# In-projection of a hybrid attention backbone: gates, keys and high parts on ScalarE instead of GpSimd

## Chip, core and metric

One core of one Trainium2 chip. The metric is the device time of one execution in microseconds (us), the median of several runs.

## What is computed

One layer of a diffusion backbone over 2048 latent tokens and 256 context tokens of width 1024, in float32. The part that matters here is the combined input projection and the gated scan (HGRN2) that reads four heads of it:

```python
p = modulate(x, norm1_g[l], sh1, sc1) @ w_in[l]
pc = modulate(ctx, norm1_g[l], csh1, csc1) @ w_in[l]

q = silu(p[..., O_HQ:O_HFF])
def gate(z, lb):
    f = lb + (1.0 - lb) * sigmoid(z)
    return 1.0 - f, log(f)
fwd = gate(p[..., O_HFF:O_HFB], lb_fb[0])
bwd = gate(p[..., O_HFB:O_HI], lb_fb[1])
```

f is the decay per token and channel, 1 - f is the key. There are two scans, one forwards and one backwards, each of four heads with 128 key channels and 64 value channels. Latent attention, a Fourier mixture, an output projection and a feed-forward network follow; they are not touched.

## The kernel before, in words

**Precision.** A float32 product is made from three TensorE products of a rounded format (mm3, lines 83 to 87): each operand is split into a high part, the rounded value, and a low part, what is left. Function hi (line 72) makes the high part, on the engine that it is given: a tensor_scalar with 1 and 0 on GpSimd (POOL), a copy on ScalarE (ACT), a copy on VectorE (DVE). Function lo (line 80) subtracts on DVE. So every weight (wraw, loaded by DMA) becomes wh and wl, and every modulated activation (xmt) becomes xh and xl.

**Stages.** The in-projection works in blocks: one of 256 context tokens (up to about 115 us in the profile), then four of 512 latent tokens (to about 898 us). For each block prep normalises the rows, transposes them on TensorE (ptx), lets ACT apply gain and shift (xmt, line 301) and splits the result, eight times for the eight slices of 128 features. The prep of the next block is emitted before the fourth head of the present one. Then come values and output gates (values_in, 512 columns), four heads (head_in, 384 columns each: query, forward gate, backward gate), the columns of attention (attention_in, 448) and of the Fourier mixture (fourier_in, 256). Weights come in pieces of at most 1536 columns of a tile (pieces, load_w): a latent block has ten pieces of 1536, two of 1344, three of 1024 and one of 896. There are two buffers of wh, two of wl and three of wraw; a new wh has to wait until TensorE has used the one before last.

**One head (hgrn).** ACT takes the sigmoids of the query and of the two gates out of PSUM. POOL then makes the gates, f = sigmoid x (1 - lb) + lb (line 369, one direction each), both keys at once, k = 1 - f (line 370, 1024 wide), and a second copy of f forwards (line 372). DVE makes q x f (line 377) and kd, the sum of the two keys (line 379). The scan over 128 tokens is then done by doubling, in seven levels m = 1, 2, 4, ... 64. In each of the first five ACT copies the keys of the level into ku (line 389), TensorE makes the level's scores psl from ku and q (line 394), and DVE puts them into pr and multiplies keys and queries by the decays of the level (lines 415 and 418), in place, for the next one. POOL multiplies the decays in pairs (tt, line 421), seven products, each half as wide as the one before. The last two levels use TensorE without a copy (pfin, lines 410 and 412). Then kt (transposed keys), pd (state increments), S (states) and po (output) follow. ACT also issues the DMAs that store dsb, q2 and ot.

**Order.** The tile framework plans the order of the instructions of each engine on its own, by the order of the program and by when it expects operands and buffers; nothing is written out by hand. Each engine works its queue in that order. In the trace the projection matmuls of the next head (accf) lie between the levels of the present one on TensorE.

**Who makes wh before.** For a latent block POOL, for the context block ACT (the argument eng of load_w). xh and the context's xch are made on POOL in both cases.

Of the kernel before, what the change touches and what calls it, by code (L numbers as in the profile page):

```python
# [13 lines left out]
AF = mybir.ActivationFunctionType  # L14
ALU = mybir.AluOpType
# [10 lines left out]
TB = 512  # L26
# [16 lines left out]
def tile_backbone(  # L43
# [6 lines left out]
    pe, act, dve, pool, sp = nc.tensor, nc.scalar, nc.vector, nc.gpsimd, nc.sync  # L50
# [21 lines left out]
    def hi(eng, dst, src):  # L72
        if eng is pool:
            pool.tensor_scalar(dst, src, 1.0, 0.0, ALU.mult, ALU.add)  # L74
        elif eng is act:
            act.copy(dst, src)  # L76
        else:
            dve.tensor_copy(dst, src)

    def lo(dst, src, h, eng=None):  # L80
        (eng or dve).tensor_tensor(dst, src, h, ALU.subtract)  # L81
# [32 lines left out]
    lbt = const.tile([P, 8], F32, name="lbt")  # L114
    omlb = const.tile([P, 8], F32, name="omlb")
# [6 lines left out]
    def rstd(rp, ssq, n, scale, name):  # L122

        m = rp.tile([P, 16], F32, tag="rs_m", name=name + "m")
        r = rp.tile([P, 16], F32, tag="rs_r", name=name + "r")
        pool.tensor_scalar(m[:, :n], ssq, scale, EPS, ALU.mult, ALU.add)
        pool.tensor_tensor(r[:, :n], m[:, :n], half[:, :n], ALU.pow)
        return r
# [94 lines left out]
    with p1 as ph:  # L223
# [17 lines left out]
        def load_raw(cols, n, k0, nk):  # L241
            raw = wp.tile([P, 1536], F32, tag="wraw", bufs=3, name="wraw")
            rv = raw[:, :nk * n].rearrange("p (k n) -> p k n", k=nk)
            o = 0
            for s, wd in cols:
                sp.dma_start(rv[:, :, o:o + wd],
                             w_in[0, k0 * P:(k0 + nk) * P, s:s + wd].rearrange("(k p) n -> p k n", p=P))
                o += wd
            return raw

        def pieces(n):
            step = min(4, 1536 // n)
            return [(k0, min(step, KT - k0)) for k0 in range(0, KT, step)]
# [7 lines left out]
            state[h] = b2.tile([P, 64], F32, tag=f"S{h}", bufs=6, name=f"S{h}_i")  # L261
            dve.memset(state[h], 0.0)

        def load_w(cols, n, k0, nk, eng):

            raw = early.pop((cols[0], k0), None)
            if raw is None:
                raw = load_raw(cols, n, k0, nk)
            wh = wp.tile([P, 1536], F32R, tag="wh", name="wh")
            wl = wp.tile([P, 1536], F32R, tag="wl", name="wl")  # L270
            hi(eng, wh[:, :nk * n], raw[:, :nk * n])
            lo(wl[:, :nk * n], raw[:, :nk * n], wh[:, :nk * n])
            return (wh[:, :nk * n].rearrange("p (k n) -> p k n", k=nk),
                    wl[:, :nk * n].rearrange("p (k n) -> p k n", k=nk))

        def prep(blk, xs):
            src, w, t0, T, bi = blk
            nt = T // P
            ssq = e2.tile([P, 4], F32, tag="ssq", name="ssq")
            for t in range(nt):  # L280
                junk = ea.tile([P, D], mybir.dt.bfloat16, tag="junk", name="junk")
                act.activation(junk, xs[t], AF.Square, accum_out=ssq[:, t:t + 1])
            r = rstd(e2, ssq[:, :nt], nt, 1.0 / D, "rx")
            for t in range(nt):
                dve.tensor_scalar(xs[t], xs[t], r[:, t:t + 1], None, ALU.mult)
            xh, xl = [], []
            per = TB // T
            bank = {}

            def step(k):  # L290
                if k % per == 0:
                    pp, tag = [(ps1, "tp"), (ps1, "ho"), (pss, "hs"), (pss, "hs")][0 if w == 0 else k // per]
                    if w == 0:
                        pp, tag = (pss, "hs") if k % 2 else (ps1, "tp")
                    bank[0] = pp.tile([P, TB], F32, tag=tag, name="ptx")
                pt = bank[0]
                po = k % per * T
                for t in range(nt):
                    pe.transpose(pt[:, po + t * P:po + (t + 1) * P], xs[t][:, k * P:(k + 1) * P], ident)
                xm = e2.tile([P, TB], F32, tag="xmt", name="xmt")  # L300
                act.activation(xm[:, :T], pt[:, po:po + T], AF.Identity, bias=modt[:, w, k:k + 1], scale=gain1[:, w, k:k + 1])
                if w == 0:
                    h = xmp.tile([P, TB], F32R, tag="xh", name="xh")
                    l = xmp.tile([P, TB], F32R, tag="xl", name="xl")
                else:
                    if k % 4 == 0:
                        bank[1] = e1.tile([P, 1024], F32R, tag=("zh", "zl")[k // 4], name="xch")
                    if k % 2 == 0 and k < 4:
                        bank[2] = e1.tile([P, 512], F32R, tag="uv", bufs=2, name="xcl")
                    if k == 4:  # L310
                        bank[2] = ea.tile([P, 1024], F32R, tag="pt", name="xcl2")
                    h = bank[1][:, k % 4 * CTX:(k % 4 + 1) * CTX]
                    l = bank[2][:, k % 2 * CTX:(k % 2 + 1) * CTX] if k < 4 else bank[2][:, (k - 4) * CTX:(k - 3) * CTX]
                hi(pool, h[:, :T], xm[:, :T])
                lo(l[:, :T], xm[:, :T], h[:, :T])
                xh.append(h)
                xl.append(l)
            return (xh, xl), [lambda k=k: step(k) for k in range(KT)]

        def token_major(xm, blk, cols):  # L320
            T = blk[3]
            n = sum(wd for _, wd in cols)
            acc = [psm.tile([P, 512], F32, tag="mm", name="acc") for _ in range(T // P)]
            for k0, nk in pieces(n):
                wh, wl = load_w(cols, n, k0, nk, pool if T == TB else act)
                for t in range(T // P):
                    for k in range(nk):
                        kk = k0 + k
                        ts = slice(t * P, (t + 1) * P)
                        mm3(acc[t][:, :n], xm[0][kk][:, ts], xm[1][kk][:, ts], wh[:, k, :], wl[:, k, :],  # L330
                            kk == 0, kk == KT - 1)
            return acc

        def feature_major(xm, blk, cols):
            T = blk[3]
            n = sum(wd for _, wd in cols)
            acc = [psm.tile([P, TB], F32, tag="mm", name="accf") for _ in range(n // P)]
            for k0, nk in pieces(n):
                wh, wl = load_w(cols, n, k0, nk, pool if T == TB else act)
                for f in range(n // P):  # L340
                    for k in range(nk):
                        kk = k0 + k
                        fs = slice(f * P, (f + 1) * P)
                        mm3(acc[f][:, :T], wh[:, k, fs], wl[:, k, fs], xm[0][kk][:, :T], xm[1][kk][:, :T],
                            kk == 0, kk == KT - 1)
            return acc

        def hgrn(blk, h, acc, vt):
            lat = blk[1] == 0
            T = blk[3]  # L350
# [8 lines left out]
            if lat:  # L359
                f3 = hp[h % 2].tile([P, 3, T], F32, tag="f3", name="f3")  # L360
                k2 = hp[h % 2].tile([P, 2, T], F32, tag="k2", name="k2")
            else:
                f3 = ea.tile([P, 2, T], F32, tag="rope", name="f3c")
                k2 = ea.tile([P, 2, T], F32, tag="junk", name="k2c")
            act.activation(f3[:, 0, :], pff[:, :T], AF.Sigmoid)
            act.activation(f3[:, 1, :], pfb[:, :T], AF.Sigmoid)
            for d in range(2):
                i = d * 4 + h
                pool.tensor_scalar(f3[:, d, :], f3[:, d, :], omlb[:, i:i + 1], lbt[:, i:i + 1], ALU.mult, ALU.add)
            pool.tensor_scalar(k2, f3[:, 0:2, :], -1.0, 1.0, ALU.mult, ALU.add)  # L370
            if lat:
                pool.tensor_scalar(f3[:, 2, :], f3[:, 0, :], 1.0, 0.0, ALU.mult, ALU.add)
                q = hp[h % 2].tile([P, T], F32, tag="q", name="q")
                act.activation(q, pq[:, :T], AF.Sigmoid)
                dve.tensor_tensor(q, pq[:, :T], q, ALU.mult)
                q2 = hp[h % 2].tile([P, 2, T], F32, tag="q2", name="q2")
                dve.tensor_tensor(q2, f3[:, 1:3, :], strided(q, 0, [[0, 2], [1, T]]), ALU.mult)
                kd = b1.tile([P, T], F32, tag="kd", name="kd")
                dve.tensor_tensor(kd, k2[:, 0, :], k2[:, 1, :], ALU.add)
                pr = b1.tile([P, TB], F32, tag="pr", name="pr")  # L380
# [196 lines left out]
        xm, steps = prep(blocks[1], x0)  # L577
# [28 lines left out]
        for n, blk in enumerate(blocks[1:]):  # L606
# [15 lines left out]
            if not end:  # L622
                xm = nxm
# [416 lines left out]
    with ExitStack() as ph:  # L1040
# [451 lines left out]
        for g, i in enumerate(begins):  # L1492
            n, ks = DORDER[g // len(DK)], DK[g % len(DK)]
# [77 lines left out]
```

## Time and profile before

| | |
|---|---|
| Median of 3 runs | 3284.93 us (3282.6 to 3285.95) |
| Profiled execution | 3281.53 us, span 3279.7 us |
| Granted TensorE clock, mean of the span | 0.982 |
| Busy: TensorE, VectorE, ScalarE, GpSimd | 95%, 65%, 37%, 24% |

In the views PE is TensorE (PEld its weight loads), DVE is VectorE, ACT is ScalarE, POOL is GpSimd. A busy time is the time in which an instruction of that engine was running. An idle time is shown in square brackets, with the instruction that ended it. "L394" is line 394 of the kernel. The granted clock is a share of 2.4 GHz; the other level is 1.2 GHz.

### The profile page before, as it was taken

Reading aid. Unit: us, or ns where it says so; the run is one execution under the profiler, and the core shown is the slowest. Engines: PE = TensorE matmul, PEld = TensorE weight load, DVE = VectorE, ACT = ScalarE, POOL = GpSimd, SP = SyncE. Lnnn points to the kernel's source line nnn. Section 1 sums busy time; section 2 is a strip of 40 time slices with the busy share of each in tenths; the row PEclk is TensorE's granted clock in tenths of the full one; section 3 lists DMA queues with packets and bytes.
Section 4 is the critical chain, followed back from the end, with each engine's and each line's share of the span. In section 5 each row is a group of like instructions: output and inputs, shape, how many; then the busy total and the mean of one; then the engine's idle time right before and its main releaser. Section 6 shows DMA issues by size and latency. Waiting matters only on the chain.

```text
span 3279.7 us, 45162 instructions
## 1 busy us (share of the span) xinstructions
PE 3101.9 (95%) x16770; PEld 2594.1 (79%) x16770; DVE 2135.6 (65%) x3354; ACT 1221.2 (37%) x2524; POOL 789.4 (24%) x784
## 2 busy tenths in 40 slices
PE   7998999999979999999999989999999999999987
PEld 5777777777758888888888877888878888888866
DVE  6675655656686767676656466766677666455765
ACT  3323122222225545555553334333343333343343
POOL 3433443424440111110101341111101111010534
PEclk9999999999989999999999989999999999999998
DMA  6523233133361212121105665533353333865562
GB/s 232 168 71 121 83 95 108 56 110 99 95 214 35 62 43 82 45 79 34 36 31 201 220 223 175 184 99 108 107 157 113 97 103 112 266 228 177 193 212 103
DMA packets 372609, 407.98 MB, mean 124 GB/s; under 512 B 50122, under 2 KB 240420, under 8 KB 371364
## 3 DMA queue, kind: packets, MB, share of 16 engines
q1 hardware_dynamic: 357748, 394.08, 37.9%
q10 hardware_dynamic: 13776, 8.92, 0.9%
q8 instruction: 132, 2.16, 0.3%
q0 software_dynamic: 864, 2.10, 0.2%
q14 instruction: 89, 0.73, 0.1%
HBM read 296.21 MB, written 108.79 MB: 123 GB/s over the span
## 4 chain that ended last, share of the span: by engine, by line
PE 53%; DMA 4%; DVE 3%; POOL 2%; ACT 1%; issue 1%; SPq 0%; POOLq 0%; DVEq 0%; ACTq 0%
PE sc L890 7%; PE dn L85 3%; PE dn L87 3%; PE dn L86 3%; PE y L87 3%; PE y L85 3%; PE y L86 3%; PE ptv L906 3%; PE z L85 2%; PE z L87 2%; PE z L86 2%; PE x L86 2%; PE x L87 2%; PE x L85 2%; PE po L87 1%; PE po L86 1%
## 5 line engine op out<-in xcount | busy, mean ns | idle before, releaser
L892 DVE TENSOR_REDUCE mx<-sc 128x1 f32<-128x512 f32 (+1 forms) x320 | 201.8, 631 | 123.0 <-PE sc L890 122.3
L1371 POOL TENSOR_TENSOR e<-e,e 128x512 f32<-128x512 f32 x44 | 91.3, 2076 | 751.1 <-ACT e L1370 689.6
L76 ACT CAST pth<-ptv 128x512 fp32r<-128x512 f32 x288 | 169.6, 593 | 234.9 <-PE ptv L906 228.2
L85 PE MATMUL dn<-wp,hdh 128*128 128x512 f32 x616 | 241.9, 393 | 6.4 <-ACT tmp L1472 5.2
L87 PE MATMUL dn<-wp,hdl 128*128 128x512 f32 x616 | 242.2, 393 | 5.0 <-DVE hdl L81 5.0
L86 PE MATMUL dn<-wp,hdh 128*128 128x512 f32 x616 | 241.4, 392 | 0.0
L81 DVE TENSOR_TENSOR ptl<-ptv,pth 128x512 fp32r<-128x512 f32 x288 | 196.2, 686 | 66.3 <-ACT pth L76 64.0
L898 ACT ACTIVATE p<-sc,mx 128x512 f32<-128x512 f32 (+1 forms) x320 | 201.9, 649 | 91.2 <-DVE mx L895 87.3
L85 PE MATMUL y<-xol,wp 128*128 128x512 f32 x528 | 207.7, 393 | 6.1 <-DVE xol L81 4.0
L86 PE MATMUL y<-xoh,wp 128*128 128x512 f32 x528 | 206.4, 391 | 0.0
L87 PE MATMUL y<-xoh,wp 128*128 128x512 f32 x528 | 205.7, 391 | 0.1
L81 DVE TENSOR_TENSOR wp<-wg,wp 128x512 fp32r<-128x512 f32 x176 | 127.3, 725 | 110.7 <-ACT wp L76 106.9
L81 DVE TENSOR_TENSOR wl<-wraw,wh 128x1536 fp32r<-128x1536 f32 (+3 forms) x78 | 118.6, 1521 | 118.5 <-POOL wh L74 117.3
L890 PE MATMUL sc<-kth,q 128*128 128x512 f32 (+1 forms) x640 | 194.6, 377 | 0.0
L87 PE MATMUL accf<-xh,wl 128*128 128x512 f32 x448 | 184.5, 412 | 10.3 <-DVE wl L81 10.3
L890 PE MATMUL sc<-kp,q 128*128 128x512 f32 (+1 forms) x640 | 190.4, 374 | 0.0
L85 PE MATMUL accf<-xl,wh 128*128 128x512 f32 x448 | 183.6, 410 | 0.0
L86 PE MATMUL accf<-xh,wh 128*128 128x512 f32 x448 | 182.9, 408 | 0.0
L906 PE MATMUL ptv<-ident,p 128*128 128x128 f32 x1152 | 178.7, 275 | 3.0 <-DVE ptl L81 1.5
L81 DVE TENSOR_TENSOR hdl<-hr,hdh 128x512 fp32r<-128x512 f32 x154 | 121.8, 803 | 84.9 <-ACT hdh L76 50.9
L85 PE MATMUL po<-ptl,ckh 128*128 128x256 f32 x576 | 169.1, 294 | 0.0
L76 ACT CAST hdh<-hr 128x512 fp32r<-128x512 f32 x154 | 94.4, 621 | 188.8 <-PE dn L86 145.0
(387 smaller groups left out, 8525.7 us busy)
## 6 DMA issues: line engine op xcount, KB each, us to landing
wg<-in_w_gate_up_dram SPq DMA_DIRECT2D x88, 512.0 KB, 4.8
hr<-hid SPq DMA_DIRECT2D x154, 256.0 KB, 3.9
wraw<-in_w_in_dram SPq DMA_DIRECT2D x112, 256.0 KB, 3.9
dw<-in_w_down_dram SPq DMA_DIRECT2D x97, 256.0 KB, 4.7
hid<-hs SPq DMA_DIRECT2D x66, 256.0 KB, 2.0
wm<-in_w_mod_dram SPq DMA_DIRECT2D x64, 256.0 KB, 2.7
hid<-e SPq DMA_DIRECT2D x44, 256.0 KB, 2.0
hid<-f SPq DMA_DIRECT2D x44, 256.0 KB, 3.3
```

Of the source, the lines that this page charges most:

```text
L76: act.copy(dst, src)
L81: (eng or dve).tensor_tensor(dst, src, h, ALU.subtract)
L85: pe.matmul(ps, ah, bl, start=first, stop=False, skip_group_check=more)
L86: pe.matmul(ps, ah, bh, start=False, stop=False, skip_group_check=more)
L87: pe.matmul(ps, al, bh, start=False, stop=last, skip_group_check=more)
L890: pe.matmul(s[:, :n], a[:, ts], bb[:, js], start=i == 0, stop=i == 4)
L892: dve.tensor_reduce(mx[:, j:j + 1], s[:, :n], AX.X, ALU.max)
L898: act.activation(u["p"][:, a:e], u["s"][i][:, :e - a], AF.Exp, bias=mx[:, 5:6], accum_out=mx[:, 6 + i:7 + i])
L906: pe.transpose(pt[:, i, u * P:(u + 1) * P], ps[u]["p"][:, (2 * g + i) * P:(2 * g + i + 1) * P], ident)
L1371: pool.tensor_tensor(e6, e6, e, ALU.add)
```

## The change

Every high part of the in-projection (wh, xh, xch), both gates, the keys and the copy of f are made by ACT, with the same values: the gates as an activation Identity with a scale and a bias per partition, the keys as Identity with scale -1 and bias 1. On POOL stay the products of the decays (tt) with their last copy, and the roots (rstd). Buffers, loads, matmuls and DVE's instructions are as before.

```diff
@@ -261,14 +261,14 @@
             state[h] = b2.tile([P, 64], F32, tag=f"S{h}", bufs=6, name=f"S{h}_i")
             dve.memset(state[h], 0.0)
 
-        def load_w(cols, n, k0, nk, eng):
+        def load_w(cols, n, k0, nk):
 
             raw = early.pop((cols[0], k0), None)
             if raw is None:
                 raw = load_raw(cols, n, k0, nk)
             wh = wp.tile([P, 1536], F32R, tag="wh", name="wh")
             wl = wp.tile([P, 1536], F32R, tag="wl", name="wl")
-            hi(eng, wh[:, :nk * n], raw[:, :nk * n])
+            hi(act, wh[:, :nk * n], raw[:, :nk * n])
             lo(wl[:, :nk * n], raw[:, :nk * n], wh[:, :nk * n])
             return (wh[:, :nk * n].rearrange("p (k n) -> p k n", k=nk),
                     wl[:, :nk * n].rearrange("p (k n) -> p k n", k=nk))
@@ -311,7 +311,7 @@
                         bank[2] = ea.tile([P, 1024], F32R, tag="pt", name="xcl2")
                     h = bank[1][:, k % 4 * CTX:(k % 4 + 1) * CTX]
                     l = bank[2][:, k % 2 * CTX:(k % 2 + 1) * CTX] if k < 4 else bank[2][:, (k - 4) * CTX:(k - 3) * CTX]
-                hi(pool, h[:, :T], xm[:, :T])
+                hi(act, h[:, :T], xm[:, :T])
                 lo(l[:, :T], xm[:, :T], h[:, :T])
                 xh.append(h)
                 xl.append(l)
@@ -322,7 +322,7 @@
             n = sum(wd for _, wd in cols)
             acc = [psm.tile([P, 512], F32, tag="mm", name="acc") for _ in range(T // P)]
             for k0, nk in pieces(n):
-                wh, wl = load_w(cols, n, k0, nk, pool if T == TB else act)
+                wh, wl = load_w(cols, n, k0, nk)
                 for t in range(T // P):
                     for k in range(nk):
                         kk = k0 + k
@@ -336,7 +336,7 @@
             n = sum(wd for _, wd in cols)
             acc = [psm.tile([P, TB], F32, tag="mm", name="accf") for _ in range(n // P)]
             for k0, nk in pieces(n):
-                wh, wl = load_w(cols, n, k0, nk, pool if T == TB else act)
+                wh, wl = load_w(cols, n, k0, nk)
                 for f in range(n // P):
                     for k in range(nk):
                         kk = k0 + k
@@ -366,10 +366,10 @@
             act.activation(f3[:, 1, :], pfb[:, :T], AF.Sigmoid)
             for d in range(2):
                 i = d * 4 + h
-                pool.tensor_scalar(f3[:, d, :], f3[:, d, :], omlb[:, i:i + 1], lbt[:, i:i + 1], ALU.mult, ALU.add)
-            pool.tensor_scalar(k2, f3[:, 0:2, :], -1.0, 1.0, ALU.mult, ALU.add)
+                act.activation(f3[:, d, :], f3[:, d, :], AF.Identity, bias=lbt[:, i:i + 1], scale=omlb[:, i:i + 1])
+            act.activation(k2, f3[:, 0:2, :], AF.Identity, bias=1.0, scale=-1.0)
             if lat:
-                pool.tensor_scalar(f3[:, 2, :], f3[:, 0, :], 1.0, 0.0, ALU.mult, ALU.add)
+                act.copy(f3[:, 2, :], f3[:, 0, :])
                 q = hp[h % 2].tile([P, T], F32, tag="q", name="q")
                 act.activation(q, pq[:, :T], AF.Sigmoid)
                 dve.tensor_tensor(q, pq[:, :T], q, ALU.mult)
```

## Rows read from the trace of the kernel before

**Rows 1.** The page, busy time of the engines (share of the span).

```profile
PE 3101.9 (95%) x16770; PEld 2594.1 (79%) x16770; DVE 2135.6 (65%) x3354; ACT 1221.2 (37%) x2524; POOL 789.4 (24%) x784
```

**Rows 2.** Stretches: busy us and count of each engine, granted clock, DMA share, GB/s.

```profile
100.00:900.00 800.00, 737.81 (x4591) 613.65 (x4589) 502.68 (x661) 193.02 (x396) 329.81 (x319) 0.98 0.34 99
...
280.00:290.00 10.00, 6.59 (x23) 4.91 (x21) 8.89 (x12) 2.61 (x4) 4.37 (x4) 0.66 0.55 176
...
350.00:360.00 10.00, 7.53 (x35) 6.10 (x35) 5.02 (x4) 1.45 (x2) 9.33 (x7) 1.00 0.40 110
...
550.00:560.00 10.00, 7.53 (x32) 6.17 (x30) 7.43 (x5) 2.39 (x4) 9.68 (x7) 0.83 0.28 79
```

**Rows 3.** TensorE's waits from 100 to 900 us: us in total, times, longest.

```profile
PE psl L394 <- ACT ku L389: 21.7, 13, 2.5
PE psl L394 <- DVE q L418: 15.6, 14, 1.8
PE accf L87 <- DVE wl L81: 10.3, 3, 3.5
PE pfin L410 <- DVE q L418: 4.0, 5, 0.9
```

**Rows 4.** All waits from 100 to 900 us, longest first.

```profile
POOL wh L74 <- PE acc L87: 148.6, 23, 24.2
...
POOL wh L74 <- PE accf L86: 92.7, 27, 6.5
...
ACT ku L389 <- POOL k L370: 60.9, 16, 5.2
```

**Rows 5.** POOL in order of time, one head: start us, us, engine, line, operation.

```profile
350.06 0.77 POOL L369 TENSOR_SCALAR f<-f,omlb,lbt 128x512 f32<-128x512 f32 x1 [4.83 <-ACT f L365]
...
351.90 1.49 POOL L74 TENSOR_SCALAR wh<-wraw 128x1536 fp32r<-128x1536 f32 x1 [0.37 <-PE accf L86]
353.37 2.34 POOL L369 TENSOR_SCALAR f<-f,omlb,lbt 128x512 f32<-128x512 f32 x1
355.80 2.08 POOL L370 TENSOR_SCALAR k<-f 128x1024 f32<-128x1024 f32 x1
357.85 1.46 POOL L421 TENSOR_TENSOR tt<-f 128x768 f32<-128x768 f32 x1
```

**Rows 6.** The same head on ACT, DVE and TensorE, in order of time.

```profile
352.07 0.60 ACT L366 ACTIVATE f<-accf 128x512 f32<-128x512 f32 x1 [2.12 <-PE accf L87]
...
353.42 1.82 DVE L81 TENSOR_TENSOR wl<-wraw,wh 128x1536 fp32r<-128x1536 f32 x1 [5.46 <-POOL wh L74]
...
355.75 1.22 DVE L377 TENSOR_TENSOR q<-f,q 128x1024 f32<-128x1024 f32 x1 [0.51 <-POOL f L369]
...
357.91 0.85 ACT L389 COPY ku<-k 128x512 f32<-128x512 f32 x1 [5.24 <-POOL k L370]
...
357.91 1.95 DVE L379 TENSOR_TENSOR kd<-k 128x512 f32<-128x512 f32 x1 [0.94 <-POOL k L370]
...
358.81 1.59 PE L394 MATMUL psl<-q,ku 128*128 128x128 f32 x8 [2.47 <-ACT ku L389]
...
364.83 0.68 DVE L418 TENSOR_TENSOR q<-q,tt 128x512 f32<-128x512 f32 x1
```

**Rows 7.** ACT's groups by shape, 0 to 960 us: busy us, mean ns, idle before.

```profile
L76 ACT CAST wh<-wraw 128x1024 fp32r<-128x1024 f32 x10 | 10.4, 1044 | 22.7 <-DMA wraw<-in_w_in_dram 17.4 <-PE accf L86 5.3
...
L76 ACT CAST wh<-wraw 128x768 fp32r<-128x768 f32 x4 | 3.3, 836 | 4.0 <-PE acc L87 2.4 <-PE accf L86 1.5
...
L301 ACT ACTIVATE xmt<-ptx,modt,gain 128x512 f32<-128x512 f32 x32 | 23.5, 776 | 35.8 <-DVE xl L81 32.7 <-PE ptx L299 2.6 <-DVE S L443 0.5
```

**Rows 8.** DVE and TensorE at the prep of the next block, in order of time.

```profile
280.53 1.55 DVE L491 TENSOR_SCALAR pt<-pt,rqr 128x256 f32<-128x256 f32 x1
...
282.26 0.34 DVE L491 TENSOR_SCALAR pt<-pt,rqr 128x256 f32<-128x256 f32 x1
...
284.38 0.80 PE L87 MATMUL accf<-xh,wl 128*128 128x512 f32 x1 [3.41 <-DVE wl L81]
```

## Prediction

> **What bounds the kernel now.** I read the page first: TensorE is busy for 95% of the span [rows 1], so time can only come back where TensorE stands still or runs slow. The change touches the in-projection alone, which lies between 100 and 900 us in the trace (its context block before that), so I went on to the table of stretches: over those 800 us TensorE is busy for 737.8, ScalarE (ACT) for 193, GpSimd (POOL) for 330 and VectorE (DVE) for 503 [rows 2]. No engine but TensorE is short of time. 62 us of TensorE are idle, and the granted clock is 0.98 in the mean, some 2% of 800 us, so 16 us more are lost to the lower of its two levels.
>
> Which waits make up the 62 us is in TensorE's own list of waits [rows 3]: the level products (psl) wait for the key copy ku on ACT, 21.7 us in 13 waits; psl and pfin wait for DVE's q products, 15.6 + 4.0 us; three times a projection waits for a low part of the weights (wl), 10.3 us. The list of all waits says what stands behind ku: ACT's 16 waits for POOL's k, 60.9 us [rows 4].
>
> One head shows the mechanism [rows 5, 6]. ACT's second sigmoid ends at 352.67. POOL has just begun a weight copy (wh, 351.90, 1.49 us), so the gate waits till 353.37. Then that gate takes 2.34 us, where the first one took 0.77 with the same shape: DVE's wl (two SBUF inputs) began at 353.42, and POOL finished only after it. The keys k take 2.08 us, half of that beside DVE's q product. At 357.88 the keys are there, ku follows, and psl starts at 358.81, after 2.47 us of idle TensorE. So the delay of the first level is POOL's queue and POOL's slow running beside DVE, and that is what the change takes out.
>
> **The change, part by part.** Durations are from the profiled execution of 3281.53 us (span 3279.7, so 1.8 us lie around it); the median of the runs is 3284.93, 3.4 above it. I work out a difference in the trace and take it off the median.
>
> *Gates and keys.* Per latent head ACT gets two gates (512 wide, scale and bias per partition, as xmt: 0.776 us [rows 7]), one key pass over 1024 (as wh 1024 wide: 1.044) and one copy of 512. The two rows of wh on ACT give 0.81 ns an element, so 512 cost 0.836 - 0.208 = 0.63 us. Behind the second sigmoid come one gate and the keys: 0.78 + 1.04 = 1.82 us, so the keys would be ready at 354.5, 3.4 us earlier; if ACT first has to do the wh copy (1536 wide: 1.044 + 512 x 0.81 ns = 1.46 us) they come at 356.0, still 1.9 earlier. psl of this level also needs DVE's q product, which stands behind wl: wl ends at 355.24, the product takes 1.22, so 356.5. psl can then start near 356.5 to 357.0 rather than 358.81: 1.8 to 2.3 us of a 2.47 gap, and all of the shorter ones. Of 21.7 us I take 19.
>
> *What is late next.* DVE. Its kd product starts at 357.91, right when the keys are there; now it could start at 356.46, when the q product ends: 1.45 us earlier. TensorE arrives up to 2.3 us earlier, so in the first head of each of the four blocks its next wait for q grows by 0.85: +3 us. In the others the two shifts are alike, or DVE gains more. Levels together: -16 us.
>
> *High parts of weights and activations.* By the code a latent block has 16 wh copies: ten of 1536, two of 1344, three of 1024, one of 896; with four blocks and 0.81 ns an element that is 85 us on ACT. 32 xh copies cost 32 x 0.63 = 20, the gates 32 x 0.78 = 25, the keys 17, the copies of f 10: 157 us on top of 193 in 800 us, 44%. The load itself is hidden by ACT's idle time; were that gone, each copy would stand in front of a ku. What the move gives is at the prep of the next block: up to 284.38 TensorE stands for 3.41 us for wl, which on DVE is queued behind the norms of queries and keys; one scaling there took 1.55 us, the next of its shape 0.34 [rows 8], and POOL was at a wh copy during the first. With POOL quiet 1.2 us go there, and some 0.7 in the products next to it (estimated from the same ratio): three such places, -6. The xl products of that stretch and the q products behind them run less slowly too: I take 1 us a block, -4.
>
> *Clock.* In 280 to 290, where the 3.41 us gap lies, the granted clock was 0.66, so much of it passed at the 1.2 GHz level; in 550 to 560 it was 0.83 with TensorE busy for 7.53 of 10 us; but 350 to 360 kept 1.00 with the same 7.53 [rows 2]. So a shorter gap may or may not give the clock back. Bounds: 0 and the whole 16 us. Since most dips lie behind gaps that go, but not all do, I take -8.
>
> *What it costs.* No DMA is moved, but ACT's queue also issues the stores of dsb, q2 and o, and these, sigmoids, ku and kt now stand behind wh copies that wait for TensorE to free a buffer. The trace has no such wait on ACT here. Below: 0, if the copy is always due when it comes up. Above: each of the 40 wide copies holds TensorE for its 1.46 us, 58 us. TensorE has projection matmuls of the next head between the levels, which cover about one copy, so I stay near the lower end: 4 copies, +6. In the context block eight copies of 256 (0.42 us each) now alternate with xmt on ACT, 3.4 us at most, part of it in ACT's waits for the transposes: +1. Fewer POOL instructions save nothing by themselves. Sum: -16 - 6 - 4 - 8 + 6 + 1 = -27, so 3258 us.
>
> **Rivals.** *The wait is handed on to DVE.* POOL keeps the decays' products (tt, 1.46 us and six smaller). In the trace DVE's kd, right beside the first of them, takes 1.95 us, a product of the same shape 0.68 when they are done [rows 5, 6]. They now start as soon as the gates are there, some 3 us earlier, onto wl and the q product; if these stretch by what kd does now (1.27), psl starts at 357.8, and with kd delayed alike the next wait eats what the first gives back. Then a head gains 1 us where the gap was 2.47 and hardly anything elsewhere, with no clock regained: 4 to 5 us in all, 3280. For it: DVE, not POOL, is behind 19.6 us of TensorE's waits [rows 3]. Against it: POOL's gates and keys are gone from the overlap. The Trainium skill ("GPSIMD Engine Reference", section Specifications) says that the two engines share their SBUF interfaces, with contention while a VectorE instruction has two SBUF inputs; by that rule this rival's overlap costs what the old one did, and the trace agrees for kd.
>
> *ACT's queue becomes the wait; slower.* POOL's wh stood 92.7 us in 27 waits for the projections of a head and 148.6 us in 23 for the other ones [rows 4]; there nothing was behind it that TensorE needed soon. On ACT a ku stands behind it. If a wh copy comes up before TensorE has freed its buffer, the ku behind it is late by the mean of those waits, 92.7 / 27 = 3.4 us, and TensorE with it. With one such hold in each of the 16 heads it is 55 us in place of my 6: -27 + 49 = +22, 3307. It decides from about ten holds, where the gain of 34 is used up. For it: one queue of ACT now carries both chains. Against it: a copy that is placed after the matmuls that free its buffer rarely waits long, and ACT is under half busy.
>
> *The change doesn't do what it says*: the order on the engines is planned anew, and the gaps come back elsewhere in equal size. Time as before, 3285.
>
> **How the numbers follow.** This kernel's measurement can tell about 0.2%, 6.6 us, from no change. Forecast: 0.66, from -50 (all 21.7, 10.3 and 16 us back) to -10. Handed on to DVE: 0.12, mostly within 0.2%, a little of it faster. ACT's queue: 0.17, slower. No effect: 0.05. Faster: 0.66 + 0.04 = 0.70; same 0.08 + 0.05 = 0.13; slower 0.17. The range goes from 3235 (-50) to 3290, which takes in the second and the fourth case and the mildest of the third, and leaves out some 0.15 above and a little below.
>
> **What would show it.** Right: ku waits for ACT's own keys for no time; TensorE's waits for ku fall from 21.7 us to under 5; idle TensorE in the in-projection falls from 62 to about 40 us, the granted clock rises; gates near 0.78 us, all alike; TensorE's waits for q near 20 us still; ACT near 350 us busy in the stage. Handed on: the waits for ku are gone and those for q have doubled. ACT's queue: TensorE waits for ku longer than before, and ku's releaser is no longer DVE's k but ACT itself, with wh waits for TensorE in front. The prediction is wrong if TensorE's idle time falls and the time does not, or if the time falls outside the in-projection.

## The result, and the profile after

The changed kernel takes 3235.96 us (median of 4 runs, 3230.5 to 3238.43) where the one before takes 3283.76 beside it (4 runs, 3280.25 to 3285.95): a ratio of 0.9843 [0.9824, 0.9862], 51.6 us of the 3284.93 that the prediction started from. The forecast was 3258, 27 us less, so the sign was right and the size was half of what came: 3233.4 by the ratio, just beyond the low end of the range, 3235. (The two medians by themselves lie 47.8 us apart, the two profiled executions 43.6.) The profiled execution of after took 3237.96 us, span 3236.2.

The page's line of busy times, against [rows 1]:

```profile
PE 3090.6 (96%) x16770; PEld 2592.0 (80%) x16770; DVE 2105.0 (65%) x3354; ACT 1376.1 (43%) x2704; POOL 564.6 (17%) x604
```

ACT has taken up 154.9 us and POOL given off 224.8; DVE, whose instructions nobody touched, is busy for 30.6 us less. That last number is the first sign of what the prediction missed.

To see where the time went I marked the same events in both traces. The first latent gate's sigmoid starts at 143.5 before and 141.7 after, the last uv of the Fourier columns at 893.8 and 839.9, the first score of the latent attention at 972.5 and 924.6, the last at 1736.8 and 1689.4; the span ends 43.5 us earlier. So 52.1 us come back between the first two marks, which I call the in-projection here, and 1.8 ahead of them; 6 are lost again in the stretch up to the scores, and some 4 after them. The two stretches (columns as in [rows 2]), of before and then of after:

```profile
143.50:893.80 750.30, 692.20 (x4354) 575.72 (x4353) 472.10 (x610) 175.81 (x350) 309.33 (x298) 0.98 0.31 91
893.80:972.50 78.70, 56.37 (x281) 44.91 (x280) 68.19 (x111) 25.57 (x48) 41.29 (x45) 0.87 0.72 210
```

```profile
141.70:839.90 698.20, 673.39 (x4338) 566.16 (x4336) 440.44 (x610) 311.50 (x495) 138.25 (x152) 1.00 0.33 96
839.90:924.60 84.70, 62.43 (x298) 50.56 (x298) 71.59 (x113) 25.98 (x49) 41.03 (x45) 0.84 0.68 205
```

In the in-projection TensorE's idle time falls from 58.1 us (750.30 - 692.20) to 24.8, by 33.3, and its busy time by 18.8. Most of the latter is clock: (1 - granted clock) x 10 us, summed over the windows of 10 us from 150 to the end of the stretch, is 17.0 us before (up to 890) and 1.7 after (up to 840), 15.3 less. Another 1.8 us were not saved but moved: the output products (po) of the last head run ahead of the last uv before, and behind it after (839.85 to 841.66), so that the stretch has 16 matmuls less. Under 2 us stay without a cause.

The 6 us behind the in-projection are not idle time either: TensorE is idle for 22.3 us there before and after. Most of them are those 1.8 us of po and the clock, which by the two rows (0.87 over 78.70 us, 0.84 over 84.70) costs some 3 us more after than before.

TensorE's waits in that stretch of after, longest first (us in total, times, longest), against [rows 3]:

```profile
PE ptx L299 <- ACT xmt L301: 7.5, 3, 2.5
PE psl L394 <- DVE q L418: 5.5, 9, 0.8
PE psl L394 <- DVE q L377: 5.3, 5, 1.1
PE psl L394 <- ACT pr L397: 3.6, 3, 1.2
...
PE pfin L410 <- DVE q L418: 1.1, 2, 0.7
```

The waits for ku (21.7) and for wl (10.3) are gone. The waits for q of L418 have fallen too, from 15.6 + 4.0 to 5.5 + 1.1. New are 5.3 us for the product q x f of L377 and 3.6 for pr; the wait for xmt grew from 2.7 to 7.5. All of psl and pfin: 41.3 us before, 15.5 after, 25.8 less. Of wl and ptx: 5.5 less. With some small ones that is the 33.3.

The head of [rows 5, 6] after the change, first ACT, then POOL, DVE and TensorE, each in order of time:

```profile
334.49 1.48 ACT L76 CAST wh<-wraw 128x1536 fp32r<-128x1536 f32 x1 [0.33 <-PE accf L86]
335.88 0.59 ACT L366 ACTIVATE f<-accf 128x512 f32<-128x512 f32 x1
336.50 0.82 ACT L369 ACTIVATE f<-f,lbt,omlb 128x512 f32<-128x512 f32 x1
337.35 1.07 ACT L370 ACTIVATE k<-f 128x1024 f32<-128x1024 f32 x1
338.44 0.86 ACT L389 COPY ku<-k 128x512 f32<-128x512 f32 x1
...
337.39 1.70 POOL L421 TENSOR_TENSOR tt<-f 128x768 f32<-128x768 f32 x1 [46.51 <-ACT f L369]
...
336.01 1.76 DVE L81 TENSOR_TENSOR wl<-wraw,wh 128x1536 fp32r<-128x1536 f32 x1 [5.41 <-ACT wh L76]
337.68 2.49 DVE L377 TENSOR_TENSOR q<-f,q 128x1024 f32<-128x1024 f32 x1
340.10 1.31 DVE L379 TENSOR_TENSOR kd<-k 128x512 f32<-128x512 f32 x1
...
340.32 1.56 PE L394 MATMUL psl<-q,ku 128*128 128x128 f32 x8 [1.10 <-DVE q L377]
```

From the start of the second sigmoid to psl it is 4.44 us, against 6.74 before [rows 6]. ku is ready at 339.30. What ends the wait is DVE: tt has gone in between wl and the q product, which takes 2.49 us in place of 1.22. TensorE stands still for 1.10 us, not 2.47.

### The profile page after: what moved, and what is told of

Same layout as the page of the kernel before. It is cut to its first block, busy times and chain, and to the rows that moved or that the text cites. A ratio compares the mean times of both kernels' runs of the same rounds, so it can differ in the third digit from the quotient of the medians.

```text
span 3236.2 us, 45208 instructions
## 1 busy us (share of the span) xinstructions
PE 3090.6 (96%) x16770; PEld 2592.0 (80%) x16770; DVE 2105.0 (65%) x3354; ACT 1376.1 (43%) x2704; POOL 564.6 (17%) x604
## 4 chain that ended last, share of the span: by engine, by line
PE 54%; DVE 3%; DMA 3%; POOL 2%; ACT 1%; issue 1%; SPq 0%; POOLq 0%; DVEq 0%; ACTq 0%
PE sc L890 7%; PE y L85 3%; PE dn L85 3%; PE y L87 3%; PE dn L87 3%; PE dn L86 3%; PE y L86 3%; PE ptv L906 3%; PE z L85 2%; PE z L87 2%; PE z L86 2%; PE x L85 2%; PE x L86 2%; PE x L87 2%; PE po L87 1%; PE po L86 1%
## 5 line engine op out<-in xcount | busy, mean ns | idle before, releaser
L81 DVE TENSOR_TENSOR hdl<-hr,hdh 128x512 fp32r<-128x512 f32 x154 | 116.8, 771 | 88.1 <-ACT hdh L76 48.4
```

## The experiments

The theory after the result: DVE gains as much as ACT does, because POOL's instructions make DVE's last longer, the weight copies above all. The rivals: all of the gain in the levels is the shorter way to the keys, as forecast; or the planner simply found a better order. The three parts alone ask which of them gives what, the two runs after them whether it is the length of a chain or POOL's work beside DVE that costs. Ratios are to the kernel before, timed on the same chip beside each version; a difference to after is that of the two ratios, times 3285, and by their intervals it is uncertain by 7 to 9 us. Stage means the in-projection between the two events above, in the profiled execution (52.1 us shorter after); that is one execution of each, not all on the same chip. Idle is TensorE's idle time in it, and what the clock costs is summed as above, up to the end of the stage (before: 58.1 and 17.0).

### The three parts, each alone

**Gates, keys and the copy of f on ACT**, the rest as before:

```diff
-pool.tensor_scalar(f3[:, d, :], f3[:, d, :], omlb[:, i:i + 1], lbt[:, i:i + 1], ALU.mult, ALU.add)
+act.activation(f3[:, d, :], f3[:, d, :], AF.Identity, bias=lbt[:, i:i + 1], scale=omlb[:, i:i + 1])
```

(and likewise k2 and the copy of f)

> Only the gates, the keys and the copy of f go to ScalarE; all high parts stay on GpSimd. Theory A (GpSimd's gate and key instructions, stretched beside VectorE, made the wait of the first level): the waits of TensorE for ku fall from 21.7 us to under 4, the three waits for wl (10.3 us) stay above 7, the time falls by 25 to 35 us of the 48 that the whole change gave. Theory B (the queue on GpSimd, where a wh copy of 1.49 us stands in front of the gates, made it): the gates no longer stand behind wh here either, so the waits for ku fall too, but weights alone on ScalarE would do the same. Theory C (VectorE is the real limit): under 10 us faster, the waits for q double.

Measured: 0.9913 [0.9894, 0.9931], 28.6 us and as expected; the stage is 25.3 us shorter, 42.0 us of it idle, 6.8 us lost to the clock. TensorE's waits:

```profile
PE psl L394 <- DVE q L418: 16.8, 19, 1.8
PE accf L87 <- DVE wl L81: 10.4, 3, 3.5
PE psl L394 <- DVE q L377: 9.1, 13, 1.4
PE pfin L410 <- DVE q L418: 3.4, 5, 0.8
```

The waits for ku are gone, and 9.1 us of new ones for the q product of L377 have come: handed on, by two fifths. The waits for q of L418 stay, as the prediction had it. So it isn't this part that shortened them.

**High parts of the weights on ACT**, the rest as before:

```diff
-hi(eng, wh[:, :nk * n], raw[:, :nk * n])
+hi(act, wh[:, :nk * n], raw[:, :nk * n])
```

> Only wh goes to ScalarE in the latent blocks; gates, keys, copy of f and the activations' high parts stay on GpSimd. Theory A: the gates on GpSimd still run beside wl on VectorE and still take near 2.3 us and the keys near 2.1, so TensorE's waits for ku stay above 12 us; the time falls by 3 to 12 us, mostly at the prep of the next block, where wh no longer runs beside the norms. Theory B: the gates start 0.7 us earlier in every head, ku's waits fall to 10 or less, and the time falls by 15 us or more. If wh copies hold ScalarE's queue (my rival of the prediction): slower by 5 us or more.

Measured: 0.9926 [0.9906, 0.9945]; the stage is 17.3 us shorter, 42.7 idle, 17.0 lost to the clock. TensorE's waits:

```profile
PE psl L394 <- ACT ku L389: 18.1, 9, 2.5
PE ptx L299 <- ACT xmt L301: 9.6, 3, 3.2
PE psl L394 <- DVE q L418: 7.9, 11, 1.6
...
PE pfin L410 <- DVE q L418: 1.7, 2, 0.9
```

24 us, and neither of the two theories fits: the waits for ku hardly moved (18.1), and yet the time fell by twice what the first one allows. The wait for wl is gone, and the wait for xmt has grown in its place (9.6, from 2.7). The waits for q have halved, from 19.6 to 9.6, with POOL's gates and keys where they were. This is the part that shortens the levels beyond ku.

The trace of before shows how. Nine of the 58 copies of wh that POOL makes in the stage lie beside a product of the levels, which then takes 1.5 to 2.0 us instead of 0.7; behind eight of these TensorE waits for q, 6.8 us in all. One of them, from before, in order of time:

```profile
367.57 1.89 POOL L74 TENSOR_SCALAR wh<-wraw 128x1536 fp32r<-128x1536 f32 x1 [2.84 <-DVE pr L399]
368.05 1.95 DVE L415 TENSOR_TENSOR k<-k,tt 128x512 f32<-128x512 f32 x1
369.92 1.75 DVE L81 TENSOR_TENSOR wl<-wraw,wh 128x1536 fp32r<-128x1536 f32 x1
...
373.02 1.13 PE L394 MATMUL psl<-q,ku 128*128 128x128 f32 x8 [0.86 <-DVE q L418]
```

The k product lost 1.27 us (1.95 against 0.68), more than the 0.86 that TensorE then stood still. With the weights on ACT none of these eight waits is left.

**High parts of the activations on ACT**, the rest as before:

```diff
-hi(pool, h[:, :T], xm[:, :T])
+hi(act, h[:, :T], xm[:, :T])
```

> Only the activations' high parts (xh, xch) go to ScalarE. Theory A: they touch only the prep of the next block and the start: xl is no longer stretched (0.93 to 0.69 us), the time falls by 2 to 10 us, the waits for ku stay near 21.7. Theory C (everything in this stage is VectorE's load): falls by 10 us or more, since xl is the only instruction that gets shorter. If ScalarE becomes the limit of the prep: slower by 3 us or more.

Measured: 0.9953 [0.9936, 0.997], some 15 us; the stage is 10.9 us shorter, 50.1 idle, 13.7 lost to the clock; the waits for ku (21.9) and wl (8.3) stay. More than expected. DVE's 24 xl of the stage took 942 ns each before and take 679 here, 6 us in all, and the waits for q are at 16.4 (12.0 + 4.4).

The three stage gains make 53.5 us, the whole change 52.1: by the stages the parts add. By the ratios they do not: 28.6, 24.3 and 15.4 make 68.3 us, the whole change 51.6. So some of what each part gives may be the same; how much stays open.

**All but the activations.** After, with their copies put back on POOL:

```diff
-hi(act, h[:, :T], xm[:, :T])
+hi(pool, h[:, :T], xm[:, :T])
```

> The changed kernel with the activations' high parts (xh, xch) back on GpSimd; gates, keys and wh stay on ScalarE. If the three parts add up (28.6 + 24.4 + 15.5 us when each was moved alone, 68 together, against 51 for all of them), this should lose 15 us against the changed kernel; if they overlap (each removes the same holds of VectorE), it loses 3 us or less. I expect 0 to 6 us slower than the changed kernel: ratio to the kernel before between 0.984 and 0.987.

Measured: 0.9876 [0.9856, 0.9896], 11 us slower than after, and 8.9 us in the stage (30.1 idle, 5.1 lost to the clock). So this part is worth something on top of the others too. The expectation was 0 to 6; by the uncertainty above 11 can't be told from 6, nor from the 15 of this part alone.

### A longer chain, and POOL's work beside DVE

**The key pass done twice.** After, with the line repeated; one more ACT instruction of 1.07 us in each head, ahead of ku:

```diff
 act.activation(k2, f3[:, 0:2, :], AF.Identity, bias=1.0, scale=-1.0)
+act.activation(k2, f3[:, 0:2, :], AF.Identity, bias=1.0, scale=-1.0)
```

> The changed kernel with the key pass of every head done twice on ScalarE (the same values into the same buffer), so the chain from the second sigmoid to the first level is 1.07 us longer in each of 16 heads, and the planner of the order knows it. Theory P (TensorE only loses what the plan did not expect: stretching beside another engine; a longer chain that is planned is filled with projection matmuls of the next head): within 5 us of the changed kernel, TensorE has some five more projection matmuls ahead of the first level's product, its gap there stays about 1.1 us. Theory L (the length of the chain is what counts): 14 to 18 us slower than the changed kernel, the gaps at the first level 1 us longer each.

Measured: 0.9828 [0.9809, 0.9847], not to be told from after; the stage is 10.4 us shorter than after's (16.6 idle). TensorE's waits (line numbers are one higher behind the new line):

```profile
PE psl L395 <- ACT pr L398: 4.2, 4, 1.1
PE psl L395 <- DVE q L419: 2.1, 5, 0.4
...
PE psl L395 <- ACT ku L390: 1.3, 4, 0.3
```

Sixteen times 1.07 us on the chain that the prediction counted cost nothing that can be told. The run says less than it was meant to, though. In after no psl waits for ku any more: the first ku of a head is ready 0.8 us or more ahead of its psl in 15 of the 16 heads, so that most of the 1.07 us fell into time in which TensorE was not waiting for ACT. In the head shown above ku comes at 340.33 (339.30 in after) and psl starts at 340.38 (340.32); TensorE stands still for 0.33 us ahead of it and not for 1.10, with 18 projection matmuls there since the second sigmoid, not 14. In the second head of each block psl starts 6.5 us behind the second sigmoid (4.6 in after), without a wait: there the order put other matmuls ahead of it. Whether POOL's 2.34 and 2.08 us in [rows 5] cost something because they were longer than the order expected, or by the plain length of the chain, no run tests. (Of the 10.4 us 2.2 are left at the end of the span; the stage's length alone is not the time.)

**POOL kept busy beside DVE.** After, with POOL copying each raw weight piece onto itself once DVE has read it (the values stay as they are). Nothing on ACT, DVE or TensorE needs POOL's copy at once:

```diff
 lo(wl[:, :nk * n], raw[:, :nk * n], wh[:, :nk * n])
+pool.tensor_scalar(raw[:, :nk * n], raw[:, :nk * n], 1.0, 0.0, ALU.mult, ALU.add)
```

> The changed kernel, and GpSimd copies every piece of raw weights onto itself once VectorE has made wl from it: as many and as long copies as the kernel before had there, but nothing in the head waits for them, only the next load of that buffer. Theory H (a GpSimd instruction and a VectorE one with two SBUF inputs exclude each other for their whole length, so each of these copies may hold VectorE up to 1.5 us in the chain of the levels): VectorE's q times f and level products show means above 1.9 and 0.75 us, TensorE's waits for q and for the q times f product grow by 10 us or more, the time grows by 8 to 25 us against the changed kernel. Theory S (GpSimd's work itself costs nothing, only its place in the chain did): within 3 us of the changed kernel.

Measured: 0.9967 [0.9955, 0.9979], 41 us slower than after: nearly the whole gain is gone (stage 732.7, idle 47.8, lost to the clock 13.6). TensorE's waits:

```profile
PE psl L395 <- DVE q L419: 23.2, 21, 2.3
...
PE pfin L411 <- DVE q L419: 4.5, 8, 0.9
```

One of the copies on POOL, and DVE beside it, in order of time:

```profile
365.63 1.47 POOL L273 TENSOR_SCALAR wraw<-wraw 128x1536 f32<-128x1536 f32 x1 [6.24 <-DVE wl L81]
...
365.46 0.73 DVE L400 COPY_PREDICATED pr<-masks,psl 128x512 f32<-128x512 uint8 x1
366.08 1.56 DVE L419 TENSOR_TENSOR q<-q,tt 128x512 f32<-128x512 f32 x1
367.57 0.68 DVE L416 TENSOR_TENSOR k<-k,tt 128x512 f32<-128x512 f32 x1
```

The q product that began during the copy took 1.56 us and ended 0.54 after it; the k product behind it, of the same shape, took 0.68. The waits for q went from 6.6 us (5.5 + 1.1) to 27.7 (23.2, and 4.5 of pfin). That is the effect by itself, though not clean in its size. The copies do not lie where the kernel before had wh: 28 of the 58 lie beside a level product (19) or a kd (9) that takes 1.1 us or more, in before nine. And tt now stands behind these copies on POOL's queue (DVE waited 2.7 us in all for tt), and the reload of a raw buffer waits for the copy (ACT's wh waited 20.2 us for its load, DVE's wl 5.4). TensorE shows no wait for wl.

**The decays' products on DVE.** After, with the last frequent work of POOL in the levels taken off it too:

```diff
-pool.tensor_tensor(nt_[:, :ns, :], ev[:, :ns, :, 0], ev[:, :ns, :, 1], ALU.mult)
+dve.tensor_tensor(nt_[:, :ns, :], ev[:, :ns, :, 0], ev[:, :ns, :, 1], ALU.mult)
```

> The changed kernel with the products of the decays (tt) on VectorE instead of GpSimd, so that GpSimd has next to nothing left in a head. Theory H: q times f falls from 1.85 to 1.23 us, kd from 1.47 to 0.69, the level products of m = 1 to near 1 us or less; VectorE gets some 2.7 us of products per head in exchange. The waits for q times f (5.3 us) go; the time changes by -8 to +3 us against the changed kernel. If VectorE's load is the limit: slower by 5 us or more, with the waits for q above 12 us.

Measured: 0.9784 [0.9764, 0.9804], 19 us faster than after, more than expected, and the fastest version of this study (3218.34 us). TensorE's waits in the stage:

```profile
PE ptx L299 <- ACT xmt L301: 7.6, 3, 2.6
PE psl L394 <- DVE q L418: 1.2, 3, 0.4
PE pfin L410 <- DVE q L418: 1.1, 2, 0.7
```

DVE's groups by shape (busy us, mean ns of one):

```profile
L377 DVE TENSOR_TENSOR q<-f,q 128x1024 f32<-128x1024 f32 x16 | 19.6, 1222 | 5.3 <-ACT f L369 5.0
...
L421 DVE TENSOR_TENSOR tt<-f 128x768 f32<-128x768 f32 x16 | 15.2, 951 | 0.0
L379 DVE TENSOR_TENSOR kd<-k 128x512 f32<-128x512 f32 x16 | 11.0, 686 | 0.0
```

DVE gets 112 products more, 42 us of work, and is busy for 446.6 us of the stage in place of 440.4: all of tt costs it 6 us, for its other products shrink by nearly as much. L377 has a mean of 1222 ns against 1846 after, kd 686 against 1467. The stage is 680.1 us with 10.7 idle, and no window of 10 us below full clock.

**The same in the kernel before** (POOL keeps wh, gates and keys, DVE makes tt):

> The kernel before with nothing changed but the products of the decays, which go to VectorE; gates, keys and high parts stay on GpSimd. Theory H (every GpSimd instruction that meets one of VectorE's makes one of the two wait): kd falls from 1.95 to 0.69, the first k product from 1.60 to 1.1, and the waits of TensorE for q from 19.6 us to under 12; but the gates and the keys on GpSimd still take near 2.3 and 2.1 us, so its waits for ku stay above 15 us. 5 to 20 us faster than the kernel before. If VectorE's load were the limit of this stage: 10 us or more slower.

Measured: 1.0012 [1.0, 1.0023]; nothing gained, where 5 to 20 us were expected. The miss has a cause that shows. TensorE's waits:

```profile
PE psl L394 <- ACT ku L389: 21.8, 13, 2.5
PE psl L394 <- DVE q L418: 15.6, 17, 1.8
```

DVE's group of kd, and then POOL and DVE in order of time in one head:

```profile
L379 DVE TENSOR_TENSOR kd<-k 128x512 f32<-128x512 f32 x16 | 11.1, 692 | 14.3 <-POOL k L370 14.3
```

```profile
364.08 1.48 POOL L74 TENSOR_SCALAR wh<-wraw 128x1536 fp32r<-128x1536 f32 x1 [9.83 <-PE accf L86]
...
364.43 1.67 DVE L418 TENSOR_TENSOR q<-q,tt 128x512 f32<-128x512 f32 x1
```

kd did shrink, from 1946 to 692 ns, and yet the waits stand as in [rows 3] (pfin's alone fell, from 4.0 to 1.0, while the clock cost 22.1 us, 5 more). The weight copy that POOL makes in the middle of the levels now holds another q product, and the keys come as late as ever. Here, with one holder left, taking away another moved the hold.

### Two more places

The copies hi(th) of the Fourier tables and hi(ch) of the normalised queries moved from POOL to ACT, alone on top of after, and together with tt on DVE:

```diff
-hi(pool, ch[:, k], cs)
+hi(act, ch[:, k], cs)
...
-hi(pool, th[:, :step], tr[:, :step])
+hi(act, th[:, :step], tr[:, :step])
```

> The changed kernel with the same idea carried to the next stage: the high parts of the cosine tables (th) and of the normalised queries (ch) on ScalarE instead of GpSimd. In that stage (85 us between the last store of the Fourier part and the first attention score) VectorE is busy for 72 us and TensorE waits 3.8 us for cl behind ch and 2.9 us for tl on GpSimd. I expect 4 to 15 us faster than the changed kernel; no gain if the loads of the tables are what counts there (DMA is busy for two thirds).

> The changed kernel with the products of the decays on VectorE and the high parts of the tables and of the normalised queries on ScalarE, both of the last two trials together. They touch different stages, so their gains against the changed kernel should add: some 20 us and 3 to 7 us, ratio to the kernel before between 0.973 and 0.979.

Measured: 0.9822 [0.9801, 0.9844] alone, not to be told from after; 0.9785 [0.9768, 0.9802] with tt, not to be told from tt alone. No gain is shown. The stretch behind the in-projection takes 80.0 us in the first profile (84.7 in after) and 81.4 in the second (83.2 with tt alone); but in the profiles of this study it lies anywhere from 79 to 86 us, so that two executions prove nothing of these copies.

## Why the prediction was too small

**Gates and keys** (19 of the 21.7 us of ku): right. The waits for ku are gone (the q product of L377 took 5.3 of them back, see below), and ACT's durations are as estimated from [rows 7]: 0.78, 0.63, 1.04 and 1.46 us against

```profile
L76 ACT CAST wh<-wraw 128x1536 fp32r<-128x1536 f32 x40 | 59.1, 1478 | 54.1 <-PE accf L86 28.9 <-PE acc L87 25.2
...
L369 ACT ACTIVATE f<-f,lbt,omlb 128x512 f32<-128x512 f32 x32 | 26.1, 816 | 0.8
...
L76 ACT CAST xh<-xmt 128x512 fp32r<-128x512 f32 x32 | 18.8, 620 | 3.9 <-PE accf L87 3.7
L370 ACT ACTIVATE k<-f 128x1024 f32<-128x1024 f32 x16 | 17.0, 1063 | 0.2
```

(ACT's groups by shape, 0 to 960 us: busy us, mean ns, idle before). Over the whole execution ACT is busy for 154.9 us more; 157 were forecast for the latent blocks.

**What is late next**: this is the step that failed. "Levels together: -16 us" let TensorE's waits for q stand near 20 us and added 3. They fell to 6.6. The step looked at DVE in the one head of [rows 5, 6] and saw only tt as what could hold it. It read the gate's 2.34 us as POOL slowed by DVE, and missed the converse, that a copy of wh on POOL holds a DVE product in the later levels where the two meet. Three runs show that: with the weights alone moved, q waits halved; with copies of the same size put back on POOL beside after, they rose to 27.7 and 41 us were lost; with gates and keys alone moved, they stayed. So the levels gave 25.8 us, not 16, even after 8.9 us of new waits for the q product of L377 and for pr. The low end of the range has the same gap: its -50 gives back the ku, wl and clock terms whole, and nothing of q.

**High parts**, -10: the wait for wl went entirely (10.3, not 6), but the wait for xmt took 4.8 back: 5.5 net. ACT makes xmt there when DVE's xl frees the buffer, and xl stands on DVE behind the norms, which wait for POOL's roots. What the products gained is in the levels' 25.8.

**Clock**, -8: some 15. Of the two bounds it was nearly the upper one. Where [rows 2] has windows at 0.66 and 0.83, after has only two below 1.00 between 150 and 840:

```profile
260.00:270.00 10.00, 7.56 (x35) 6.03 (x34) 5.48 (x14) 5.92 (x19) 3.43 (x4) 0.98 0.61 169
270.00:280.00 10.00, 9.60 (x45) 8.15 (x46) 6.87 (x11) 8.09 (x13) 0.00 (x0) 0.85 0.82 264
```

There TensorE stood for 2.44 us up to 269.88. Seven of the eight dips of before come behind gaps of 2.4 to 3.5 us, the eighth behind one of 1.5; after has three gaps of over 2.4 us left, and one dip. It is no rule: after's gaps of 2.55 and 2.54 us, up to 455.72 and 639.92, left the clock at 1.00, as the one of 2.47 in [rows 6] did, and with the weights alone moved three windows are low (from 190, 610 and 820) where no gap over 1.6 us lies.

**What it costs**, +6 for holds in ACT's queue and +1 in the context block: none was seen, and the first latent gate came 1.8 us earlier. ACT's wh does wait for TensorE:

```profile
ACT wh L76 <- PE acc L87: 54.0, 14, 7.1
```

but no psl waits for a ku behind it; the order places it where nothing is due soon. The rival that made ACT's queue the wait has nothing for it. (Its sign takes DVE's k for what released ku; for the ku of the first level it was POOL's, [rows 4].)

Put together: -27, 9.8 more in the levels, 4.5 less at the prep, 7.3 more by clock and 8.8 more by costs that did not come make -48.4, of the 53.9 up to the end of the stage; 2.0 us of small waits, the 1.8 of po that only moved and 1.7 without a cause are the rest. Some 10 of it are given back behind the stage in that profile, the 1.8 of po among them, where the prediction had no change. So the levels are the largest miss, but not the only one: the costs and the clock were mis-sized by nearly as much.

**Handed on to DVE** was half true: its place and its form were right, the q product stretched by 1.27 beside tt in that very head, and psl waits for it 5 times, 5.3 us in all. Its size was wrong, since with wh gone from POOL the other products got shorter. It takes tt off POOL to undo it, and that gave 19 us more. The prediction priced the overlap for tt alone. The Trainium skill ("SBUF — State Buffer", section SBUF: two separate sides) calls the pair of ports that the two engines share an exclusive lock, which the one that starts first keeps for its whole instruction, where the VectorE one has two SBUF inputs and the GpSimd one reads SBUF. The pairs in the last section agree with that, but for one gate.

That a better order is part of it is not excluded, since each edit is planned anew. But the waits for q follow POOL's copies in both directions, off POOL and back onto it, and in the trace of before they stand right behind the products that lay beside a copy.

## What to carry to other kernels

Where VectorE carries a chain that TensorE waits for, count GpSimd's instructions not by GpSimd's own load but by the VectorE products that they lie beside: here a copy of 1.5 to 1.9 us cost a product of 0.68 us up to 1.3 us more, and ScalarE, which showed no such effect, was the place for it. Take all of the holders away: one alone may give nothing (1.0012 for tt in the kernel before), and the same edit 19 us once the others are gone. And before you count the length of a chain, see which operand comes last: 1.07 us more on one that was ready early cost nothing that could be told.

## What was unexpected in the hardware

In the pairs below a DVE product with two inputs in SBUF and an instruction on POOL do not share the time: one goes first at its own length, and the other ends nearly its own length after it, some 0.14 us less each time. In before, kd of 357.91 ended at 359.86, 0.55 after tt (359.31); alone it takes 0.69. The keys on POOL ended 0.91 after DVE's q product (356.97) [rows 5, 6]; alone they take 1.06, the shortest with the weights on ACT. In after the q product ended at 340.17, 1.08 after tt (339.09), alone 1.22; tt itself ended 1.32 after wl (337.77). In the run with POOL's extra copies the q product ended 0.54 after the copy, alone 0.68, while pr beside the same copy, with one input in PSUM, took its usual 0.73. One row doesn't fit: the gate of [rows 5] began 0.05 us ahead of wl by the trace, and yet it ended last, 0.47 behind it; alone it takes 0.77. ACT has none of this: 32 gates between 812 and 829 ns, whatever DVE and POOL did.
